# Two tiles of the key and value expansion in one double bank of PSUM

## Chip, cores and metric

The kernel runs on one core of a Trainium2 chip. The metric is the device time of one execution in microseconds (us). The kernel before takes 885.75 us, the median of three runs (884.52 to 885.99).

## What is computed

The reference is one step of a hybrid layer over 512 latent tokens and 128 context tokens, with a mLSTM head group (4 heads) and an attention head group (8 heads) side by side, then an output projection and an MLP. The part that the change touches is the expansion of the low-rank latent `ckv` (256 columns) to the keys and values of all eight attention heads:

```python
kv = (ckv @ w_kv_up).reshape(B, T, A_HEADS, A_NOPE + A_VDIM)
k_nope, v = kv[..., :A_NOPE], kv[..., A_NOPE:]
...
k = _rmsnorm(k, k_head_g)
```

It is done for the latent tokens, for a cache of 128 past tokens and for the context tokens: 768 rows, that is 6 blocks of 128.

## The kernel before

All of the kernel is one function, `hybrid_layer`, built with tile pools. A pool has a fixed number of buffers for each tag; a tile takes one, and the buffer comes free when every instruction that uses the tile is done. The tile framework puts in the semaphores, and it sets the order of each engine's instructions itself: by program order as priority, but an instruction that isn't ready in its own timeline (`schedule_with_timeline_sim=True`, line 1407) lets later ones go first. So the program text is not the order on the engines, and that order is fixed before the kernel runs.

**PSUM.** The pool `psd` (line 69, tag "d", function `psD`) has two buffers of 128x1024 f32, each two banks of 512. The pool `pss` (line 70, `psS`) has four buffers of one bank.

**The stages in program order.** The input projections (`group_n`, lines 490 to 506) accumulate five row blocks at once: blocks 0 and 1 are the two halves of one `psD` tile, blocks 2 and 3 those of another, block 4 is a `psS` tile. Then the four mLSTM heads follow (lines 794 to 798): `head_in` projects a head's queries, keys and gate; `mlstm` makes scores `s` and `c`, weights `W` and `p`, and numerators `n` (line 702); `mlstm_end` normalises and transposes (`den`, `hm`, `ht`, lines 766 to 790). Lines 801 to 814 transpose `ckv` into the split operands `kth` and `ktl`.

**The expansion** (lines 834 to 863) runs over two halves `hf` of the heads, and in each over six row blocks `i`. A tile `kvu{hf}{i}` takes six matmuls of 128x512 (line 846, through `mm3`, lines 486 to 488). Three readers empty it: ScalarE copies the keys to `kn` (line 848), ScalarE casts the values to `v` (line 109), VectorE subtracts to give the low part of `v` (line 110), while for the sixth block ScalarE's copy of the values to `vctx` (line 852) stands in place of the last two. ScalarE squares the keys (`sqk`, line 854) and VectorE sums them (`ssk`, line 855); both read only the copy. After the six blocks, VectorE takes the reciprocal root (lines 856 to 858) and GpSimd scales the keys (lines 860 and 861). The text below writes tile 3 for block 3 of the first half and tile h3 for block 3 of the second half. Each tile asks for a whole `psD` buffer of two banks and uses the first 512 columns.

The second half's value tile `v` (line 837) takes the SBUF buffer of `mv_u`, which the last mLSTM head still reads, so its casts can start only when the last `n` matmul is done.

**After it**, `qlt` (lines 867 to 873) transposes the query latent in three `psD` tiles, which ScalarE scales and casts; then come the query expansion `qu`, the conditioning products `ada`, attention (`head_q`, `head_k` and so on), the output projection and the MLP (`up`, `dn`). The first product of the MLP's first pair (lines 1223 to 1266) again puts two results, M1 and M2, in the halves of one `psD` tile: M1 is written and copied out by ScalarE (line 1256), and M2 is written into the other half by later matmuls.

Of the kernel before, what the change touches and what calls it, by code (L numbers as in the profile page):

```python
# [54 lines left out]
def hybrid_layer(ctx: ExitStack, tc: tile.TileContext, d, o):  # L55
# [19 lines left out]
    def U(name, dt=F32):  # L75
        return upool.tile([P, UNIT], dt, tag="u", name=name)
# [4 lines left out]
    def view(t, off, *shape):  # L81
        n = int(np.prod(shape))
        v = t[:, off:off + n]
        if len(shape) == 1:
            return v
        names = "abcd"[:len(shape)]
        return v.rearrange("p (%s) -> p %s" % (" ".join(names), " ".join(names)), **dict(zip(names, shape)))
# [5 lines left out]
    def Pp(name, dt=F32, n=T):  # L93
        return tp.tile([P, 646], dt, tag="pp", name=name, bufs=2)[:, :n]

    def sm(name, shape, dt=F32, bufs=2):
        return sp.tile(shape, dt, tag=name, name=name, bufs=bufs)

    def psD(name):
        return psd.tile([P, 1024], F32, tag="d", name=name)  # L100
# [7 lines left out]
    def split(hi, lo, src, eng=V):  # L108
        S.copy(hi, src)  # L109
        return eng.tensor_tensor(out=lo, in0=src, in1=f(hi), op=ALU.subtract)  # L110
# [89 lines left out]
    def wget(key, ahead=3):  # L200
        i = state["get"]
        assert chunks[i][0] == key, (chunks[i][0], key)
        wsplit(i + 1)
        wdma(i + 4)
        wsplit(i + ahead)
        state["get"] += 1
        return ready.pop(i)
# [137 lines left out]
    for what in ORD:  # L345
        if what == "x":
            i = state["x"]
# [15 lines left out]
    def rsqrt_v(y, x):  # L363

        n = x.shape[-1]
        t = sm("nwt", [P, 24], bufs=1)[:, :n]
        V.tensor_scalar(out=y.bitcast(I32), in0=x.bitcast(I32), scalar1=-0.5, scalar2=float(0x5F3759DF), op0=ALU.mult, op1=ALU.add)
        V.tensor_scalar(out=x, in0=x, scalar1=-0.5, scalar2=None, op0=ALU.mult)
        for _ in range(3):
            V.tensor_tensor(out=t, in0=y, in1=y, op=ALU.mult)  # L370
            V.tensor_tensor(out=t, in0=t, in1=x, op=ALU.mult)
            V.scalar_tensor_tensor(out=y, in0=t, scalar=1.5, in1=y, op0=ALU.add, op1=ALU.mult)
# [112 lines left out]
    def mm3(out, lh, ll, rh, rl, start, stop):  # L485
        PE.matmul(out, lhsT=lh, rhs=rh, start=start, stop=False)
        PE.matmul(out, lhsT=lh, rhs=rl, start=False, stop=False)
        PE.matmul(out, lhsT=ll, rhs=rh, start=False, stop=stop)
# [345 lines left out]
    for hf in range(2):  # L834
        ku = U(f"kn{hf}")
        kn = view(ku, 0, 6, 4, QK)
        vu = U(f"v{hf}", F32R)
        vv = view(vu, 0, 5, 4, P)
        hi, lo = wget(("kup", hf))
        ssk = sm("ssk", [P, 6, 4], bufs=1)  # L840
        rsk = sm("rsk", [P, 6, 4], bufs=1)
        for i in range(6):
            ps = psD(f"kvu{hf}{i}")[:, 0:512]
            for k in range(2):
                c = slice(k * 512, (k + 1) * 512)
                mm3(ps, kth[:, k, i * P:(i + 1) * P], ktl[:, k, i * P:(i + 1) * P], hi[:, c], lo[:, c], k == 0, k == 1)
            p4 = ps.rearrange("p (h c) -> p h c", h=4)
            S.copy(kn[:, i, :, 0:NOPE], p4[:, :, 0:NOPE])
            if i < 5:
                split(vv[:, i, :, 0:VD], vv[:, i, :, VD:P], p4[:, :, NOPE:P])  # L850
            else:
                S.copy(vctx[:, hf], p4[:, :, NOPE:P])
            sq = view(Pp(f"sqk{hf}{i}"), 0, 4, NOPE)
            S.activation(out=sq, in_=kn[:, i, :, 0:NOPE], func=AF.Square)
            V.tensor_reduce(out=ssk[:, i, :], in_=sq, axis=AX.X, op=ALU.add)
        V.tensor_tensor(out=ssk, in0=ssk, in1=ssr.unsqueeze(2).broadcast_to([P, 6, 4]), op=ALU.add)
        V.tensor_scalar(out=ssk, in0=ssk, scalar1=1.0 / QK, scalar2=EPS, op0=ALU.mult, op1=ALU.add)
        rsqrt_v(rsk.rearrange("p a b -> p (a b)"), ssk.rearrange("p a b -> p (a b)"))
        for k in range(4):
            G.tensor_tensor(out=kn[:, :, k, 0:NOPE], in0=kn[:, :, k, 0:NOPE], in1=rsk[:, :, k:k + 1].broadcast_to([P, 6, NOPE]), op=ALU.mult)  # L860
            G.tensor_tensor(out=kn[:, :, k, NOPE:QK], in0=krr, in1=rsk[:, :, k:k + 1].broadcast_to([P, 6, ROPE]), op=ALU.mult)
        kn_u.append(kn)
        v_u.append(vv)
# [10 lines left out]
    for hf in range(2):  # L874
# [4 lines left out]
        for i in range(NT):  # L879
            ps = (psS if i % 2 else psD)(f"qu{hf}{i}")  # L880
# [276 lines left out]
    for m in OUT_ORDER:  # L1157
        if m == 0:
            ps = ps_first
            with tc.issue_after(factors.ins):  # L1160
                mmT(ps, w_first, MHv, MLv, KT, 4)
        elif m == OUT_ORDER[1]:
            ps = psD(f"wo{m}")
# [4 lines left out]
        else:  # L1168
            ps = psD(f"wo{m}")
# [113 lines left out]
    for g in range(NG):  # L1283
# [19 lines left out]
        for h, m2 in downs(g):  # L1303
            w = wnext(("down", h, m2))
            for m in (2 * m2, 2 * m2 + 1):
                ps = psD(f"dn{h}{m}")
# [108 lines left out]
```

## Time and profile before

| what | value |
|---|---|
| median of three runs | 885.75 us |
| the profiled execution | 885.93 us |
| its span, first to last instruction | 883.8 us |
| TensorE busy | 856.6 us, 97% |
| VectorE busy | 615.9 us, 70% |
| ScalarE busy | 436.6 us, 49% |
| GpSimd busy | 297.2 us, 34% |
| expansion, first to last matmul start | 229.4 to 261.9 us |

The table is read against the span: the 2.13 us between span and execution lie around the program. Matmuls overlap, so the busy time of TensorE is an upper view of its work; what counts for the change is where TensorE stands idle, and which event ends the idle time.

### The profile page before, as it was taken

The page shows a single profiled execution, that of the slowest core. Times are in us where ns is not written, and L with a number is a line of the kernel's source. Part 1 is how long each engine was busy: PE and PEld are TensorE (multiplying, and loading weights), DVE is VectorE, ACT ScalarE, POOL GpSimd, SP SyncE. Part 2 cuts the span into 40 slices and gives each one's busy share as a digit, 9 for nine tenths or more (in the row PEclk, how much of TensorE's full clock was granted, in tenths as well). Part 3 has the DMA queues.
Part 4 walks back from the last instruction along what each step waited for, and adds up shares of the span by engine and source line. Part 5 has one row for each costly group of instructions (what it writes and reads, how often), then busy time and mean ns, then how long its engine had stood idle before and what let it go on. Part 6 is the DMA issues. An engine that isn't in the chain of part 4 may idle for free.

```text
span 883.8 us, 15202 instructions
## 1 busy us (share of the span) xinstructions
PE 856.6 (97%) x5805; PEld 801.8 (91%) x5805; DVE 615.9 (70%) x1226; ACT 436.6 (49%) x959; POOL 297.2 (34%) x301
## 2 busy tenths in 40 slices
PE   6999999999889999999989999999999999999998
PEld 5689889999778677889989999999999999999998
DVE  2654733646787889977898587595876949678663
ACT  3424425545864688955557253361544517254540
POOL 3100113322333576743753152241514215152300
PEclk9999999999999999999999999999999999999999
DMA  9742853231316200322141312122122221412132
GB/s 358 307 145 61 281 185 89 63 102 48 99 57 239 96 1 1 120 72 72 49 144 45 99 49 96 49 96 96 49 96 88 80 73 57 134 50 73 48 102 90
DMA packets 22328, 89.63 MB, mean 101 GB/s; under 512 B 3144, under 2 KB 3944, under 8 KB 18928
## 3 DMA queue, kind: packets, MB, share of 16 engines
q1 hardware_dynamic: 19440, 81.95, 26.8%
q0 software_dynamic: 1664, 4.26, 1.7%
q10 hardware_dynamic: 1152, 2.46, 0.7%
q8 instruction: 46, 0.75, 0.4%
q14 instruction: 26, 0.21, 0.1%
HBM read 85.33 MB, written 3.32 MB: 100 GB/s over the span
## 4 chain that ended last, share of the span: by engine, by line
PE 84%; DVE 8%; DMA 3%; ACT 3%; issue 1%; POOL 0%; SPq 0%; DVEq 0%; ACTq 0%; POOLq 0%
PE dn L637 25%; PE qk L637 6%; PE wo L637 5%; PE mo L637 3%; PE ada L389 2%; PE pv L1013 2%; DMA st<-in_w_ada 2%; PE n L702 2%; PE up8M L1235 1%; PE up12M L1235 1%; PE up13M L1235 1%; PE up15M L1235 1%; PE up14M L1235 1%; PE up11M L1235 1%; PE up9M L1235 1%; PE up7M L1235 1%
## 5 line engine op out<-in xcount | busy, mean ns | idle before, releaser
L109 ACT CAST wh<-st 128x1024 fp32r<-128x1024 f32 (+4 forms) x69 | 69.3, 1007 | 101.1 <-PE dn L637 32.9
L1118 DVE SCALAR_TENSOR_TENSOR xr<-dn,modT,xr 128x320 f32<-128x320 f32 x64 | 35.3, 551 | 107.3 <-PE dn L637 107.3
L637 PE MATMUL dn<-fh,wh 128*128 128x320 f32 x448 | 102.7, 310 | 0.2 <-ACT fh L1278 0.2
L110 DVE TENSOR_TENSOR wl<-st,wh 128x1024 fp32r<-128x1024 f32 (+4 forms) x67 | 83.3, 1246 | 27.8 <-ACT wh L109 26.8
L637 PE MATMUL dn<-fh,wl 128*128 128x320 f32 x448 | 102.0, 309 | 0.0
L637 PE MATMUL dn<-fl,wh 128*128 128x320 f32 x448 | 98.7, 309 | 0.0
L109 ACT CAST wu<-S 128x512 fp32r<-128x512 f32 x64 | 38.1, 616 | 98.5 <-issue 92.3
L637 PEld LDWEIGHTS dn<-fh,wh 128*128 128x128 f32 x448 | 74.8, 188 | 2.1 <-PE dn L637 1.6
L637 PEld LDWEIGHTS dn<-fh,wl 128*128 128x128 f32 x448 | 75.0, 188 | 0.0
L637 PEld LDWEIGHTS dn<-fl,wh 128*128 128x128 f32 x448 | 74.1, 188 | 0.0
L1273 POOL TENSOR_TENSOR r<-r,rbs 128x320 f32<-128x320 f32 x32 | 37.4, 1180 | 106.9 <-DVE r L1251 106.9
L110 DVE TENSOR_TENSOR wu<-S,wu 128x512 fp32r<-128x512 f32 x64 | 57.4, 906 | 1.1 <-ACT wu L109 0.9
L1277 ACT ACTIVATE r<-r 128x192 f32<-128x192 f32 (+2 forms) x96 | 40.8, 465 | 26.0 <-DVE r L1251 17.1
L729 POOL TENSOR_TENSOR W<-ngb,mask 128x128 f32<-128x128 f32 x40 | 19.5, 501 | 66.5 <-DVE p L739 33.2
L1280 DVE TENSOR_TENSOR fl<-r,fh 128x320 fp32r<-128x320 f32 x56 | 38.1, 699 | 3.0 <-ACT r L1279 3.0
L1004 POOL TENSOR_TENSOR tot<-tot,p 128x512 f32<-128x512 f32 x24 | 37.2, 1550 | 5.9 <-ACT p L986 3.9
L109 ACT CAST wu<-pair 128x512 fp32r<-128x512 f32 x24 | 14.1, 615 | 43.8 <-PE dn L637 41.6
L110 DVE TENSOR_TENSOR pu<-p,pu 128x512 fp32r<-128x512 f32 x32 | 33.0, 1046 | 2.5 <-ACT pu L109 2.5
L219 POOL TENSOR_TENSOR S<-st,st 128x512 f32<-128x512 f32 x8 | 13.0, 1627 | 60.1 <-DVE wu L110 60.1
L1013 PE MATMUL pv<-pu,v 128*128 128x512 f32 x80 | 29.1, 427 | 2.1 <-DVE pu L110 2.0
L637 PE MATMUL wo<-mh,wh 128*128 128x320 f32 x128 | 29.6, 311 | 0.7 <-DVE xr L1120 0.7
L637 PE MATMUL qk<-hh,wl 128*128 128x320 f32 x128 | 29.9, 312 | 0.0
(487 smaller groups left out, 2437.6 us busy)
## 6 DMA issues: line engine op xcount, KB each, us to landing
st<-in_w_ada SPq DMA_DIRECT2D x16, 1024.0 KB, 5.4
st<-in_w_down SPq DMA_DIRECT2D x32, 512.0 KB, 3.4
ad<-in_w_ada SPq DMA_DIRECT2D x8, 1024.0 KB, 17.2
st<-in_w_up SPq DMA_DIRECT2D x16, 512.0 KB, 3.7
pair<-in_w_up SPq DMA_DIRECT2D x16, 512.0 KB, 4.9
st<-in_w_qko SPq DMA_DIRECT2D x12, 512.0 KB, 3.6
st<-in_w_out SPq DMA_DIRECT2D x8, 512.0 KB, 3.5
x<-in_x SPq DMA_DIRECT2D x4, 640.0 KB, 6.8
```

The lines of the kernel that those rows point to most:

```text
L109: S.copy(hi, src)
L110: return eng.tensor_tensor(out=lo, in0=src, in1=f(hi), op=ALU.subtract)
L389: PE.matmul(ps[32 * j:32 * j + 32, 0:n], lhsT=sz[:, 2 * q + k, :], rhs=w[:, k, c], start=q == 0, stop=q == 3, tile_position=(0, 32 * j))
L637: PE.matmul(out[:, hf * 512:hf * 512 + HT], lhsT=wt[:, c], rhs=xt[k][:, hf * HT:(hf + 1) * HT], start=k0 == 0 and n == 0, stop=k1 == nk an ...
L729: G.tensor_tensor(out=W[:, dg:dg + P], in0=nb_[dr][:, j * P:(j + 1) * P], in1=mask[:, dr, :], op=ALU.add)
L1004: G.tensor_tensor(out=tot[h], in0=first, in1=pj, op=ALU.add)
L1013: PE.matmul(pacc[h], lhsT=v_u[hf][:, j, hh_, :], rhs=w, start=j == 0 and k == 0, stop=j == 4 and k == 1)
L1118: V.scalar_tensor_tensor(out=xr[m][:, 0:HT], in0=ps[:, 0:HT], scalar=modT[:, gi_ + m, 0:1], in1=xr[m][:, 0:HT], op0=ALU.mult, op1=ALU.add)
L1235: PE.matmul(ps, lhsT=w[:, c], rhs=b[k], start=k == 0 and w is hi and b is bh, stop=k == 3 and w is lo)
L1273: E.tensor_tensor(out=t, in0=t, in1=rbs[:, c], op=ALU.mult)
L1277: S.activation(out=t[:, c0:c1], in_=t[:, c0:c1], func=AF.Relu, bias=r[n][:, w:w + 1])
L1280: V.tensor_tensor(out=FL[n][:, c], in0=t, in1=f(FH[n][:, c]), op=ALU.subtract)
```

## The change

Two consecutive row blocks take the two halves of one `psD` tile. The matmuls, the readers and their number stay as they are, and no load, store or SBUF tile is touched.

```diff
         for i in range(6):
-            ps = psD(f"kvu{hf}{i}")[:, 0:512]
+            if i % 2 == 0:
+                pair = psD(f"kvu{hf}{i}")
+            ps = pair[:, i % 2 * 512:i % 2 * 512 + 512]
             for k in range(2):
```

## Rows read from the trace of the kernel before

**Rows 1.** The page, part 1: busy time and share of the span.
```profile
PE 856.6 (97%) x5805; PEld 801.8 (91%) x5805; DVE 615.9 (70%) x1226; ACT 436.6 (49%) x959; POOL 297.2 (34%) x301
```

**Rows 2.** The waits of TensorE: us in total, times, longest us.
```profile
PE kvu L486 <- DVE v L110: 2.8, 3, 1.3
...
PE up0M L1235 <- ACT r L1256: 1.6, 1, 1.6
```

**Rows 3.** The timeline of TensorE: start us, us, instruction, [idle before <-releaser].
```profile
234.36 0.49 PE L760 MATMUL pc<-mv_u,kw 128*128 128x129 f32 x2 [1.41 <-ACT kw L757]
...
241.79 0.50 PE L486 MATMUL kvu<-wh,kth 128*128 128x512 f32 x1 [1.26 <-DVE v L110]
...
255.59 0.50 PE L486 MATMUL kvu<-wh,kth 128*128 128x512 f32 x1 [0.93 <-DVE v L110]
...
259.28 0.50 PE L486 MATMUL kvu<-wh,kth 128*128 128x512 f32 x1 [0.65 <-DVE v L110]
...
260.78 0.39 PE L486 MATMUL kvu<-wh,kth 128*128 128x512 f32 x1
...
262.16 0.74 PE L870 MATMUL qlt<-ident,ql_u 128*128 128x128 f32 x5
...
264.80 0.77 PE L870 MATMUL qlt<-ident,ql_u 128*128 128x128 f32 x5 [0.64 <-ACT qlt L872]
...
290.86 0.84 PE L937 MATMUL Tk<-ident,kn 128*96 128x128 f32 x6
```

**Rows 4.** The timeline around the first projection, TensorE and VectorE, tile `mv`.
```profile
57.38 0.40 PE L488 MATMUL mv<-wh,hl 128*128 128x512 f32 x1
...
58.08 0.40 PE L488 MATMUL mv<-wh,hl 128*128 128x512 f32 x1
...
58.52 3.28 DVE L514 COPY mv_u<-mv 128x512 f32<-128x512 f32 x5 [0.97 <-PE mv L488]
```

**Rows 5.** The timeline around the second projection, TensorE and VectorE, tile `kv`.
```profile
74.03 0.30 PE L488 MATMUL kv<-wh,hl 128*128 128x304 f32 x1
...
74.45 0.30 PE L488 MATMUL kv<-wh,hl 128*128 128x304 f32 x1
...
74.79 0.47 DVE L531 COPY kvs<-kv 128x304 f32<-128x304 f32 x1 [1.10 <-PE kv L488]
...
75.81 0.86 DVE L531 COPY kvs<-kv 128x304 f32<-128x304 f32 x2 [0.18 <-ACT ck_u L532]
```

**Rows 6.** The timeline at the MLP's first pair, ScalarE and TensorE.
```profile
452.58 0.43 ACT L1256 COPY r<-up0M 128x322 f32<-128x322 f32 x1
...
453.06 1.74 PE L1235 MATMUL up0M<-B,wu 128*128 128x322 f32 x10 [1.60 <-ACT r L1256]
```

**Rows 7.** The timeline of VectorE in the second half of the expansion.
```profile
255.93 0.41 DVE L110 TENSOR_TENSOR v<-kvu,v 128x256 fp32r<-128x256 f32 x1
...
259.46 0.42 DVE L110 TENSOR_TENSOR v<-kvu,v 128x256 fp32r<-128x256 f32 x1
...
261.66 0.42 DVE L110 TENSOR_TENSOR v<-kvu,v 128x256 fp32r<-128x256 f32 x1 [0.72 <-ACT v L109]
...
262.33 1.06 DVE L787 TENSOR_SCALAR hm<-hm,rsh 128x128 f32<-128x128 f32 x5
```

**Rows 8.** The timeline of ScalarE in the same stretch and just behind it.
```profile
254.69 0.65 ACT L109 CAST v<-kvu 128x256 fp32r<-128x256 f32 x2 [2.98 <-PE n L702]
...
260.98 0.37 ACT L848 COPY kn<-kvu 128x256 f32<-128x256 f32 x1 [0.24 <-PE kvu L488]
261.25 0.38 ACT L109 CAST v<-kvu 128x256 fp32r<-128x256 f32 x1
...
263.95 0.80 ACT L872 ACTIVATE qlt<-qlt,small 128x640 f32<-128x640 f32 x1
264.77 0.73 ACT L109 CAST qth<-qlt 128x640 fp32r<-128x640 f32 x1
```

**Rows 9.** The timeline of GpSimd: the last scaling of the first half's keys.
```profile
255.94 0.51 POOL L861 TENSOR_TENSOR kn<-krr,rsk 128x192 f32<-128x192 f32 x1
```

## The prediction

> **What bounds the kernel now.** I read the page first: TensorE is busy for 856.6 of 883.8 us [rows 1], so an edit elsewhere pays only where it shortens one of TensorE's idle stretches. The list of TensorE's waits comes next. One of its largest entries belongs to the tiles of the change: three waits of 2.8 us together, ended by VectorE's subtraction of `v` [rows 2]. The timeline places them: 1.26 us ahead of 241.79, 0.93 ahead of 255.59, 0.65 ahead of 259.28. Two neighbours belong to the same stretch: 1.41 us ahead of 234.36, where TensorE waits for ScalarE's `kw` with two tiles of the expansion waiting to be emptied and no buffer for a third, and 0.64 ahead of the third `qlt` [rows 3]. That is 4.89 us of idle time, 0.55% of the run, and everything the edit could reach directly. A difference under about 0.2% (1.8 us) can't be told from no change in a measurement of this kernel.
>
> Before the change, two tiles are under way at most: tile i starts when tile i-2 has been read for the last time. The waits above are that rule at work.
>
> **The change, part by part.** It adds and removes no matmul, copy, cast, subtraction or DMA, so each queue has the same work. What it alters is who waits for whom. Two buffers of two halves could hold four tiles; whether four are ever under way hangs on one question: may TensorE write one half of a `psD` tile while ScalarE or VectorE reads the other half? Three places of this kernel already use the halves that way.
>
> First, the `mv` projection. In its last round each row block takes three matmuls, block 0 before block 1, the two being halves of one tile. Block 0's last matmul ends at 57.38 + 0.40 = 57.78, block 1's at 58.08 + 0.40 = 58.48. VectorE has been idle for 0.97 us and starts to read block 0 at 58.52 [rows 4], 0.74 us after its half was complete and 0.04 after the other half was. Second, `kv`: block 0 is complete at 74.33, block 1 at 74.75, and VectorE's read of block 0 starts at 74.79; its read of block 1 waits for ScalarE's read of block 0 [rows 5]. Third, and nearest to the case: M2 of the MLP's first pair is written into the half beside M1, and TensorE stands for 1.60 us until ScalarE's copy of M1 ends at 453.01, then starts at 453.06 [rows 6]. In all three the wait goes by the whole tile, not by the half: a read waits for writes to the other half, a read for a read of it, a write for a read of it.
>
> So tile 1 can't start beside the emptying of tile 0; it waits for all three of tile 0's readers, because they come earlier in the program and use the same `psD` tile. Each buffer becomes a chain, one of tiles 0, 1, 4, 5, the other of 2, 3, h0, h1, with h2, h3 behind 5 and h4, h5 behind h1. Within a chain one tile is written or emptied at a time. Two chains, so two tiles under way, as before. The engines take ready work out of program order, so I expect 0, 2, 1, 3, 4, h0, 5, h2 where it was 0, 1, 2, 3, 4, 5, h0, h1: the k-th tile waits for the emptying of the (k-2)th in both.
>
> The Trainium skill says otherwise: PSUM — Partial Sum Buffer, section "PSUM bank collisions raise a hardware error", asks for semaphores by bank and quadrant, and different banks don't collide. By that rule the two halves would be independent and four tiles could be under way; the rows of the three places speak against it for this kernel's waits.
>
> Now the terms. **Waits of 1.41, 1.26, 0.93 and 0.65 us:** each keeps its cause, with another tile in the role. Ahead of 234.36 tiles 0 and 2 are in flight in place of 0 and 1. At 241.79 it is h0 that waits for tile 3's subtraction. At 255.59 h1 waits for h0's, at 259.28 h4 for h1's. Term: 0.
>
> **The end of the second half.** Here the order can't be made up for. Before, h5 followed h4 without a gap, at 260.78. Now both are in one chain and nothing of the expansion is left beside them. h5 waits for h4's readers: keys copied at 260.98, values cast at 261.25 [rows 8], subtraction at 261.66 to 262.08 [rows 7]; h5 starts at about 262.12, 1.34 us late. The other buffer is free by then, since h3's subtraction ends at 259.88 [rows 7], so the first `qlt` moves ahead of h5 and its 0.74 us fill part of the gap [rows 3]. Left: +0.60. In return, by the time of the third `qlt` its buffer is free and ScalarE has done the first `qlt` long before, so its wait of 0.64 goes: -0.64. Together 0.0 us on TensorE's path.
>
> **What moves behind cover.** Tile 5 is written one place later (1.4 us), and so the first half's keys are scaled later than 255.94 + 0.51 = 256.45 [rows 9]. Their first reader is the transpose at 290.86 [rows 3]: 34 us of cover. If that were gone, the cost would be the 1.4 us. Loads are issued when TensorE or ScalarE frees their tiles, and those times move by tenths. Cost: 0.
>
> **What the trace doesn't show:** the new order itself, which is drawn up anew for all of the kernel behind the edit. Best case: the freer choice between tile 5 and h0 covers the 1.26 us. Worst case: no `qlt` ahead of h5, and 1.34 us. I take neither, being so close to zero on both sides, and keep -1.3 and +1.4 for the range.
>
> Sum: 885.93 for the profiled execution (span 883.8 and 2.13 around it) + 0.0 = 885.9; the median of the runs lies 0.18 lower, so 885.8.
>
> **The rivals.**
>
> *Faster: the halves are independent after all.* Then four tiles are under way. Tiles 2 and 3 fill the 1.41 us and the second half gets two tiles more ahead of the end of the mLSTM at 254.69 [rows 8]: 2 x 1.38 us of work (260.78 to 262.16) against 1.41 + 1.26 idle, so that end moves by 0.09. After it the last pair waits for h0 and h1 to be emptied, until 255.93 + 0.41 = 256.34 [rows 7], then takes 1.50 + 1.38 and ends at about 259.2 + 0.1 instead of 262.16. It saves 2.8 us: 882.9. For it: the 4.9 us are real, and the halves hold separate accumulations. Against it: the three places in rows 4 to 6. The skill's rule of the page named above would lead here. Chance 0.13.
>
> *Slower: the last pair stands alone behind other work.* If ScalarE takes the first `qlt`'s two operations, 0.80 + 0.73 us [rows 8], ahead of h4's cast, then h4's subtraction becomes ready 1.5 us later, after 263.1, and falls behind the five `hm` operations that VectorE runs from 262.33 to 263.39 [rows 7]. It then ends at 263.81 and h5 starts at 263.85 instead of 260.78: 3.07 us late, less the 0.74 of the moved `qlt`, so +2.3 us: 888.1. It decides as soon as the cast of h4 is queued behind the first of those ScalarE operations. For it: in the profile before, the subtractions of h2 and h3 already queue among such work. Against it: the cast belongs to earlier program text and has priority when it is ready. Chance 0.18.
>
> *The forecast: the change doesn't do what it says*, and two tiles remain under way. Chance 0.69.
>
> **How the numbers follow.** The likeliest case gives 885.8. With its bounds of -1.3 and +1.4, and some 0.3 for the measurement, it covers 884.2 to 887.5, which leaves out the faster rival at 882.9 and the slower one at 888.1, apart from partial cases of either, and little of the likeliest. The chances of faster by over 0.2%, no difference and slower by over 0.2% are those of the three cases.
>
> **What would show it.** In the profile after, the second tile of a pair should start only after the subtraction of the first: odd tiles' first matmuls 0.05 us or so behind VectorE's `v`, tiles 0 and 2 ahead of 1, the waits on `v` still near 2.8 us and one more ahead of h5, the `pc` wait still 1.4 us, and a first `qlt` ahead of the last expansion tile. I am wrong if four tiles' matmuls stand together at 229 to 236 us and the wait for `kw` is gone, or if the time between the last `n` matmul and the first `qu` shrinks by over 2 us.

## The result and the profile after

The changed kernel takes 892.54 us (median of 4 runs, 891.70 to 895.17), the kernel before beside it 885.87: a ratio of 1.0084 with a 95% interval of 1.0064 to 1.0104. Measured twice more it was 1.0062 (1.0042 to 1.0083) and 1.0044 (1.0027 to 1.0061). The forecast was 885.8, no change, with a range of 884.2 to 887.5; the change costs 4 to 7 us. Part of the width of that figure is TensorE's granted clock: in some traces it is at half for a few microseconds in the MLP's first pair, and some runs of every kernel here have a lower mean clock (0.990 to 0.996). The last batch of experiments is about that.

The page of the profiled execution (892.2 us, span 890.2 us), part 1, against [rows 1]:

```profile
PE 860.3 (97%) x5805; PEld 804.4 (90%) x5805; DVE 616.7 (69%) x1226; ACT 436.5 (49%) x959; POOL 296.7 (33%) x301
```

The counts are the same to the instruction, so no work was added; 6.4 us of span were. The list of TensorE's waits (us in total, times, longest) answers to [rows 2]:

```profile
PE kvu L486 <- DVE v L110: 5.3, 5, 1.6
...
PE up0M L1237 <- ACT r L1258: 2.1, 1, 2.1
```

The waits for VectorE's `v` went from three of 2.8 us together to five of 5.3. TensorE's timeline (start us, us, instruction, [idle before <-releaser]; lines behind the edit are two higher than before) shows which, against [rows 3]:

```profile
234.75 0.49 PE L760 MATMUL pc<-mv_u,kw 128*128 128x129 f32 x2 [1.41 <-ACT kw L757]
...
239.87 0.50 PE L486 MATMUL kvu<-wh,kth 128*128 128x512 f32 x1 [0.34 <-DVE v L110]
...
242.75 0.50 PE L486 MATMUL kvu<-wh,kth 128*128 128x512 f32 x1 [1.22 <-DVE v L110]
...
256.77 0.49 PE L486 MATMUL kvu<-wh,kth 128*128 128x512 f32 x1 [1.57 <-DVE v L110]
...
261.38 0.50 PE L486 MATMUL kvu<-wh,kth 128*128 128x512 f32 x1 [1.57 <-DVE v L110]
...
262.87 0.71 PE L872 MATMUL qlt<-ident,ql_u 128*128 128x128 f32 x5
264.23 0.50 PE L486 MATMUL kvu<-wh,kth 128*128 128x512 f32 x1 [0.65 <-DVE v L110]
...
266.62 0.77 PE L872 MATMUL qlt<-ident,ql_u 128*128 128x128 f32 x5 [0.19 <-ACT vctx L854]
...
268.36 0.77 PE L872 MATMUL qlt<-ident,ql_u 128*128 128x128 f32 x5 [0.97 <-ACT qlt L874]
```

The rows don't number the tiles; by the chains of the prediction, and by whose reader ends each wait, what stands ahead is in order of time: `pc`, with two tiles in flight (1.41, as before), 4 and h0 (0.34 + 1.22 for the 1.26 of before), h1 (1.57 for 0.93), h4 (1.57 for 0.65), h5 (0.65, new), and the second and third `qlt` (0.19 + 0.97 for 0.64). That is 3.0 us more idle time; a wait of 0.21 ahead of an `n` matmul at 252.16 is gone, so 2.8 us are left. I measure all kernels from here on by two ways in their traces: **the short way**, from the start of the first `kvu` matmul to that of the first `qu` matmul (36.14 us before, 265.55 - 229.41; 39.33 after), and **the long way**, to the first `up0M` matmul of the MLP (217.01 before, 220.84 after). What runs ahead of the first `kvu` is the same program in both and differs by up to 2.6 us from trace to trace.

The larger part of the growth, 1.56 us, is at h1 and h4, whose waits have the cause that the prediction named: the subtraction of the tile before them in the chain. VectorE's timeline shows why they are longer:

```profile
255.56 0.82 DVE L770 SCALAR_TENSOR_TENSOR den<-num 128x5 f32<-128x5 f32 x1
256.31 0.41 DVE L110 TENSOR_TENSOR v<-kvu,v 128x256 fp32r<-128x256 f32 x1
...
257.36 2.32 DVE L779 TENSOR_SCALAR hm<-num,den 128x128 f32<-128x128 f32 x5
259.60 1.39 DVE L780 SCALAR_TENSOR_TENSOR hm<-num,den,hm 128x128 f32<-128x128 f32 x5
260.91 0.41 DVE L110 TENSOR_TENSOR v<-kvu,v 128x256 fp32r<-128x256 f32 x1
```

The subtraction that h1 waits for stands behind `den`, which takes 0.82 us. The five `hm` products take 2.32 us. In the kernel before the same two take 0.18 and 1.07:

```profile
255.02 0.18 DVE L770 SCALAR_TENSOR_TENSOR den<-num 128x5 f32<-128x5 f32 x1
...
256.50 1.07 DVE L779 TENSOR_SCALAR hm<-num,den 128x128 f32<-128x128 f32 x5
```

The subtraction of `v` that h4 waits for is queued behind the products. And beside all of them, from 254.25 to 259.40, GpSimd now scales the first half's keys, which before was over at 256.45 [rows 9]:

```profile
254.25 0.84 POOL L862 TENSOR_TENSOR kn<-kn,rsk 128x384 f32<-128x384 f32 x1 [3.48 <-issue]
...
258.88 0.52 POOL L863 TENSOR_TENSOR kn<-krr,rsk 128x192 f32<-128x192 f32 x1
```

GpSimd's own instructions are no longer than before (0.84 and 0.51 to 0.52 us). Only VectorE pays. Taken one by one, the five products last 0.36, 0.56, 0.88, 0.56 and 0.28 us, and each of the first four ends 0.08 us behind the end of a GpSimd instruction; the third, for one:

```profile
258.08 0.84 POOL L862 TENSOR_TENSOR kn<-kn,rsk 128x384 f32<-128x384 f32 x1
258.12 0.88 DVE L779 TENSOR_SCALAR hm<-num,den 128x128 f32<-128x128 f32 x1
```

### The profile page after: what moved, and what is told of

Read it like the earlier page. It is cut to its first block, busy times and chain, and to the rows that moved or that the text cites. A ratio compares the mean times of both kernels' runs of the same rounds, so it can differ in the third digit from the quotient of the medians.

```text
span 890.2 us, 15198 instructions
## 1 busy us (share of the span) xinstructions
PE 860.3 (97%) x5805; PEld 804.4 (90%) x5805; DVE 616.7 (69%) x1226; ACT 436.5 (49%) x959; POOL 296.7 (33%) x301
## 4 chain that ended last, share of the span: by engine, by line
PE 82%; DVE 8%; DMA 4%; ACT 3%; issue 2%; POOL 0%; SPq 0%; DVEq 0%; POOLq 0%; ACTq 0%
PE dn L637 25%; PE qk L637 6%; PE wo L637 5%; PE mo L637 2%; DMA st<-in_w_ada 2%; PE ada L389 2%; PE pv L1015 2%; PE n L702 2%; PE up1M L1237 2%; PE up12M L1237 1%; PE up8M L1237 1%; PE up14M L1237 1%; PE up11M L1237 1%; PE up7M L1237 1%; PE up5M L1237 1%
## 5 line engine op out<-in xcount | busy, mean ns | idle before, releaser
L110 DVE TENSOR_TENSOR wu<-S,wu 128x512 fp32r<-128x512 f32 x64 | 59.4, 937 | 2.4 <-ACT wu L109 2.2
```

## The experiments

Theory S: the scaling, which by the later tile 5 starts 2.6 us later (24.46 us behind the first `kvu` in place of 21.90), falls beside VectorE's `hm` products and makes them slow, which holds up h1 and h4; the end of the second half costs the rest. Theory C: the chains of tiles themselves, or the order of the work, cost it. Theory K: the change itself brings the half clock in the MLP's first pair, and that is a good part of the loss. All figures in one table; ratios are to the kernel before on the same chip.

| kernel | short way | long way | five `hm` | median, us | ratio (95%) |
|---|---|---|---|---|---|
| before | 36.14 | 217.01 | 1.07 | 885.87 | 1 |
| after | 39.33 | 220.84 | 2.32 | 892.54 | 1.0084 (1.0064-1.0104) |
| e1_pair_no_scale | 37.79 | 219.30 | 1.07 | 888.30 | 1.0026 (1.0007-1.0045) |
| e2_before_no_scale | 35.76 | 216.07 | 1.07 | 885.63 | 0.9993 (0.9979-1.0008) |
| e3_pair_first_half | 37.89 | 218.52 | 2.32 | 887.04 | 1.0013 (0.9990-1.0035) |
| e4_pair_second_half | 37.59 | 219.42 | 1.07 | 887.36 | 1.0024 (1.0005-1.0042) |
| e10_pair_again | 39.14 | 220.69 | 2.32 | 892.45 | 1.0062 (1.0042-1.0083) |
| e11_pair_late_scale | 37.55 | 219.02 | 1.07 | 887.81 | 1.0019 (1.0003-1.0036) |
| e5_four_banks | 42.47 | 225.70 | 1.06 | 893.31 | 1.0077 (1.0055-1.0099) |
| e8_before_up_apart | 36.15 | 217.24 | 1.07 | 890.71 | 1.0046 (1.0031-1.0061) |
| e15_before_delay | 37.89 | 219.01 | 2.42 | 888.12 | 1.0025 (1.0009-1.0041) |
| e12_before_late_scale | 35.23 | 215.63 | 1.07 | 884.64 | 0.9986 (0.9968-1.0005) |
| e14_four_late | 38.59 | 222.00 | 1.06 | 891.22 | 1.0067 (1.0042-1.0093) |
| e16_pair_late_sep | 36.00 | 219.21 | 1.07 | 887.31 | 1.0011 (0.9997-1.0025) |
| e17_pair_third | 39.22 | 221.88 | 2.32 | 890.11 | 1.0044 (1.0027-1.0061) |
| e19_pair_late_again | 37.68 | 219.22 | 1.07 | 887.98 | 1.0023 (1.0006-1.0041) |
| e18_late_again | 35.25 | 216.72 | 1.07 | 884.86 | 0.9972 (0.9958-0.9987) |

The two ways are of one trace each. Where a program was traced again, the short way repeats within 0.2 us (after, e10 and e17; e11 and e19; e12 and e18), the long way only within 1.2 us (220.69 to 221.88 for the changed kernel), since TensorE's waits for loads of `in_w_ada` differ. So tenths count in the short way and not in the long one.

### Without the first half's scaling

Left out of the changed kernel (e1) and, as a control, of the one before (e2); the first half's keys stay unscaled in both:

```diff
-        for k in range(4):
+        for k in range(4 if hf else 0):
             G.tensor_tensor(out=kn[:, :, k, 0:NOPE], ...)
```

> The changed kernel with the first half's key scaling on GpSimd left out (eight operations); the order on TensorE is that of the changed kernel. Theory S (the scaling came later and now runs into VectorE's work behind the mLSTM): the five hm operations fall from 2.32 to about 1.07 us, the wait ahead of h1 from 1.57 to about 0.9, ahead of h4 from 1.57 to about 0.6; the way from the first expansion matmul to the first qu matmul is 1.3 to 1.7 us shorter than the 39.3 of the changed kernel. Theory C (the chain inside a pair alone costs the time): those waits stay near 1.57 and the way stays at 39.3. Time by S about 891, by C 892.5.

> The same eight operations left out of the kernel before: the control. Theory S: there the scaling ended at 256.4, ahead of the hm operations, and met only two small operations of VectorE; so the way from the first expansion matmul to the first qu matmul, 36.1 us, falls by 0 to 0.5. Time 885.4 to 885.9. Were it to fall by 1.5 too, leaving out the work would be worth that in itself and the first experiment would say nothing of the change.

```profile
256.25 1.07 DVE L779 TENSOR_SCALAR hm<-num,den 128x128 f32<-128x128 f32 x5
```

In e1 `hm` is back at 1.07, and the short way is 1.54 us less than after's, as S had it. In e2 the way falls by 0.38: the kernel before already had a little of the same neighbourhood. Between e1 and e2 there are still 2.03 us, so of the change's 3.19 us the scaling accounts for 1.16 net. The waits in the roles of h1 and h4 are the same in e1 and e2 (0.92 and 0.24). What e1 has more than e2 stands mostly ahead of h5 (0.96 us, while after has 0.65 and e2 none) and ahead of the two `qlt` (0.19 + 0.97 against 0.48).

### Pairs in one half only

```diff
-            if i % 2 == 0:
+            if i % 2 == 0 or hf == 1:    # e4: hf == 0
                 pair = psD(f"kvu{hf}{i}")
-            ps = pair[:, i % 2 * 512:i % 2 * 512 + 512]
+            h_ = 0 if hf == 1 else i % 2 * 512
+            ps = pair[:, h_:h_ + 512]
```

> Pairs in the first half only. Theory S: tile 5 is chained behind tile 4, the scaling is late and meets the hm operations, so this half of the change carries the two long waits: the way from the first expansion matmul to the first qu matmul is 38.0 to 38.6 us (before 36.1, changed 39.3), time 887.8 to 888.5 if nothing else follows. Theory C: the chain costs where no other tile is left, at the end of the second half, which is unpaired here: 36.1 to 36.5 us, time about 886.

> Pairs in the second half only. Theory S: the scaling is as early as before; only the wait of 0.65 ahead of h5 and some 0.3 at the query transposes remain: the way from the first expansion matmul to the first qu matmul is 36.9 to 37.3 us, time about 887 if nothing follows. Theory C: this half carries the loss: 38.5 to 39.3 us, 888.5 to 889. Theory K (the other half of the loss comes from the lower clock at the MLP's first pair, and from the order behind the expansion, which is here that of the changed kernel): 2 us more in either case, with a stretch at 0.5 of the full clock near 459 us.

```profile
261.68 0.50 PE L486 MATMUL kvu<-wh,kth 128*128 128x512 f32 x1 [0.65 <-DVE v L110]
...
265.80 0.77 PE L873 MATMUL qlt<-ident,ql_u 128*128 128x128 f32 x5 [0.97 <-ACT qlt L875]
```

The rows are of e4. The two halves are two separate losses: +1.75 us of short way for the first, +1.45 for the second, 3.20 together, and the whole change has 3.19. Only the first has the slow `hm`; only the second has the late h5 and `qlt`. The second costs more than S had (36.9 to 37.3 us) and less than C had (38.5 to 39.3). By the times each alone is near the edge of what can be measured.

### The scaling moved, with all of the work kept

```diff
+    ssk2 = sm("ssk", [P, 2, 6, 4], bufs=1)
+    rsk2 = sm("rsk", [P, 2, 6, 4], bufs=1)
     for hf in range(2):
...
-        V.tensor_scalar(out=ssk, in0=ssk, ...)
-        rsqrt_v(rsk..., ssk...)
...
+    V.tensor_scalar(out=ssk2, in0=ssk2, ...)
+    rsqrt_v(rsk2..., ssk2...)
+    for hf in range(2):
+        kn, rsk = kn_u[hf], rsk2[:, hf]
         for k in range(4):
             G.tensor_tensor(out=kn[:, :, k, 0:NOPE], ...)
```

> The changed kernel itself once more, beside the others on one chip. By theory S (the stage pays by itself) the way from the first matmul of the expansion to the first of the query expansion is 39.3 us, 3.2 above the kernel before, the stretch behind it up to the first up0M 0.6 us longer, and the median 3.8 us above before: a ratio of 1.0043; a granted clock of half in the first MLP pair comes in some of its runs as in some of before's, and adds some 3 us only there. By rival K (the change itself brings the half clock, by the longer wait ahead of the second part of up0M) nearly all of its runs have it, and the ratio is 1.007 or more.

> The changed kernel with all of its work, but both halves' key scaling stands behind the second half, on one inverse root for both; GpSimd scales nothing while VectorE runs the five hm operations. By theory S they take 1.07 us again in place of 2.32, the waits ahead of h1 and h4 fall from 1.57 each to about 0.9 and 0.2 to 0.7, and the way from the first kvu to the first qu is 37.6 to 38.0, as where the scaling was left out (37.8). If what was left out helped by something else than the neighbourhood of the scaling and hm, the way stays at 39 or more. GpSimd then works until some 7 us later than before, by about 287 us, and the keys are first read at about 291: no cost by that.

e10 is the changed kernel once more, e11 the same with the edit. The edit moves VectorE's reciprocal root along with GpSimd's scaling, so it takes a little more out of the stage than e1 does. Late scaling takes 1.6 to 1.8 us off the changed kernel's short way (39.14 and 39.33 against 37.55), and 4.6 us off its median on the same chip, part of which is clock (below). VectorE of e11 in the stretch of the slow group, then TensorE at h1, h4 and h5:

```profile
257.03 1.07 DVE L779 TENSOR_SCALAR hm<-num,den 128x128 f32<-128x128 f32 x5
258.02 1.40 DVE L780 SCALAR_TENSOR_TENSOR hm<-num,den,hm 128x128 f32<-128x128 f32 x5
259.33 0.42 DVE L110 TENSOR_TENSOR v<-kvu,v 128x256 fp32r<-128x256 f32 x1
```

```profile
256.51 0.50 PE L486 MATMUL kvu<-wh,kth 128*128 128x512 f32 x1 [0.92 <-DVE v L110]
...
259.81 0.50 PE L486 MATMUL kvu<-wh,kth 128*128 128x512 f32 x1 [0.24 <-DVE v L110]
...
262.97 0.50 PE L486 MATMUL kvu<-wh,kth 128*128 128x512 f32 x1 [0.95 <-DVE v L110]
```

The wait ahead of h4 is 0.24, less than the 0.65 of before; h5's has grown to 0.95. Both are as in e1, where the root had stayed in its place. The rest of the change's price stands at the end of the second half.

### The same neighbourhood made in the kernel before

If S is right, the slow `hm` can be made without any pair. Six extra scalings of the rotary part (overwritten with the same values) push the end of the eight back by some 3 us:

```diff
+        for k in ((0, 1, 2, 3, 0, 1) if hf == 0 else ()):
+            G.tensor_tensor(out=kn[:, :, k, NOPE:QK], in0=krr, ...)
         for k in range(4):
```

> The kernel before, TensorE's order and all tiles as they were, with one thing put in: GpSimd scales the rotary part of the first half's keys for six heads more (overwritten by the same values), 6 x 0.52 = 3.1 us, ahead of the eight scalings, which so fall at about 254.3 to 259.5 as in the changed kernel. By theory S the five hm operations take about 2.3 us in place of 1.07, the waits ahead of h1 and h4 grow to about 1.6 each, and the way from the first kvu to the first qu is 37.3 to 38.0 in place of 36.1. If the chain of tiles made them slow, and not GpSimd's neighbourhood, hm stays at 1.07 and the way at 36.1 to 36.3.

GpSimd, then VectorE, then TensorE of e15:

```profile
256.18 1.00 POOL L860 TENSOR_TENSOR kn<-krr,rsk 128x192 f32<-128x192 f32 x2
257.14 1.95 POOL L863 TENSOR_TENSOR kn<-krr,rsk 128x192 f32<-128x192 f32 x4
```

```profile
256.75 2.42 DVE L779 TENSOR_SCALAR hm<-num,den 128x128 f32<-128x128 f32 x5
259.09 1.39 DVE L780 SCALAR_TENSOR_TENSOR hm<-num,den,hm 128x128 f32<-128x128 f32 x5
```

```profile
255.84 0.50 PE L486 MATMUL kvu<-wh,kth 128*128 128x512 f32 x1 [1.35 <-DVE v L110]
...
260.87 0.50 PE L486 MATMUL kvu<-wh,kth 128*128 128x512 f32 x1 [1.98 <-DVE v L110]
```

The order on TensorE and the tiles are those of before, and `hm` takes 2.42 us. It ends at 259.17, 0.08 us behind GpSimd's last scaling (257.14 + 1.95 = 259.09), and the next VectorE group, 1.39 us, is as before. The short way grows by 1.75, the long by 2.00, the median by 2.06. This is the clearest of the runs: GpSimd's neighbourhood alone, without a pair, costs as much as pairs in the first half do (e3).

The Trainium skill has the rule for it, in SBUF — State Buffer, section "Who interferes with whom": VectorE and GpSimd share one pair of ports as an exclusive lock, `tensor_scalar` can enter a mode that takes it, and whoever issues first blocks the other for the whole instruction. The traces agree: products of 0.28 us each became up to 0.88 us in the changed kernel and end 0.08 us behind GpSimd's instructions, which kept their 0.84 us. The ports themselves are seen in no trace here.

### Four tiles under way

What the change was to allow, without a shared tile: four buffers of one bank each (e5), and the same with late scaling (e14). To make room, the pool `psd` is closed ahead of the stage and opened anew behind it.

```diff
+    psd_stack.close()
+    psk = kv_stack.enter_context(tc.tile_pool(name="psk", bufs=4, space=PSUM))
...
-            ps = psD(f"kvu{hf}{i}")[:, 0:512]
+            ps = psk.tile([P, 512], F32, tag="k", name=f"kvu{hf}{i}")
...
+    kv_stack.close()
+    psd = ctx.enter_context(tc.tile_pool(name="psd2", bufs=2, space=PSUM))
```

> The kernel before with four tiles of one bank each for the expansion in place of two of two banks: what the change was to allow, without a shared tile. If four under way are worth what the faster rival of the prediction said, tiles 0 to 3 run in one block, the 1.41 ahead of pc and the 0.65 ahead of h4 go, and the way from the first kvu to the first qu is 33.3, 2.8 less than before: a ratio of 0.997. If the emptying of more tiles at once puts copies and subtractions ahead of the mLSTM's own operations on ScalarE and VectorE, the wait for kw and the second half's end move out by as much, and the way is 35.5 to 37: a ratio of 1.000 at best.

> Four tiles of one bank each together with the late scaling: what four under way bring when GpSimd scales nothing beside VectorE. If the 42.5 us of the four tiles alone came from the scaling beside the hm operations (3.20 in place of 1.06) and from the half clock behind the 4.29 us for which TensorE then stood, both go and the way is 36.5 to 37.5. If the emptying of more tiles ahead of the mLSTM's own operations is what held TensorE up, it still stands for 2 us or more ahead of ht, and the way is 38 or more. To be worth its making it would have to be under 36.1.

Four tiles do run as one block, and the waits of 1.41 ahead of `pc` and 1.26 ahead of the fifth tile are gone. It is slower all the same, by 6.3 us of short way in e5, more than either expectation had, and 2.5 in e14. TensorE of e14, where the gaps are, and ScalarE from its first copy of a tile to the last of the five `dg` sums that `hm` waits for:

```profile
250.93 1.12 PE L789 MATMUL ht<-ident,hm 128*128 128x128 f32 x4 [3.74 <-DVE hm L788]
...
265.52 1.31 PE L879 MATMUL qlt<-ident,ql_u 128*128 128x128 f32 x10 [0.92 <-ACT vctx L857]
```

```profile
235.67 0.37 ACT L853 COPY kn<-kvu 128x256 f32<-128x256 f32 x1 [4.25 <-PE kvu L489]
...
246.78 0.77 ACT L853 COPY kn<-kvu 128x256 f32<-128x256 f32 x2
...
247.61 0.52 ACT L853 COPY kn<-kvu 128x256 f32<-128x256 f32 x1
...
248.47 0.46 ACT L782 ACTIVATE dg<-hm 128x128 f32<-128x128 f32 x1
```

With more tiles to empty, ScalarE puts their copies and squares among the third head's `dg` sums; the last of these starts 17.9 us behind the first `kvu` (248.47 - 230.55), against 11.8 before (241.16 - 229.41). A part of that is a later start: the four tiles' last matmuls stand together at the end of the block, and ScalarE's first copy comes 5.1 us behind the first `kvu`, against 2.8 before (232.21 - 229.41). TensorE runs ahead with the expansion and then stands for the mLSTM. In e5 it was worse, since GpSimd's scaling also fell beside the five products at L788 (3.20 us for 1.06).

Two more things cost time in these kernels. Behind the gap the granted clock was lower, 0.72 from 248 to 254 us in e14 and 0.53 and 0.62 from 248 to 260 us in e5; in all other traces it is 1.00 from 224 to 272 us. (A matmul of `s` takes 0.63 us there in e14 and 0.40 behind it.) And the first `qlt` starts only behind the last tile's `vctx`: the waits from there to the first `qu` are 0.92 + 0.71 + 0.83 us in e14, against 0.64 before. So the faster rival of the prediction, in this form, would not have been fast either. How much of the loss is the number of buffers, and how much the order inside the block, the clock and the pool opened anew, no run separates.

### M1 and M2 in tiles of their own

```diff
-        two_ = dict(M1="M2", M6="M7", M4="M3")
+        two_ = dict(M6="M7", M4="M3")
```

> The kernel before, with M1 and M2 of the first MLP pair in a tile of one bank each in place of the two halves of one tile. If waits go by the whole tile, as the prediction read from this place, the wait of 0.9 to 1.6 us for ScalarE's r ahead of the second part of up0M goes, and the time falls by 1 to 1.6 us: a ratio of 0.9985. If the wait was for something else that r stands for, it stays. If the half clock in this pair follows that wait, no run of this kernel has it, and the median falls by up to 3 us more; if not, it comes in some runs as before.

The wait for ScalarE's copy `r` [rows 6] is gone from the list, so it was a wait for the whole tile. Nothing is gained, against the expected 0.9985: TensorE takes other work first and then stands longer, at another place, and the granted clock, 1.00 up to 462 us and 0.91 from there to 468, was 0.52 in the 6 us that follow (0.50 is 1.2 GHz of 2.4):

```profile
467.99 2.25 PE L1235 MATMUL up0M<-B,wu 128*128 128x322 f32 x7 [3.46 <-DVE r L1251]
```

### Late scaling alone, and the last tile apart

e12 is the kernel before with late scaling. e16 is e11 with the last tile in a buffer of its own:

```diff
-            if i % 2 == 0:
+            if i % 2 == 0 or hf * 6 + i == 11:
                 pair = psD(f"kvu{hf}{i}")
-            ps = pair[:, i % 2 * 512:i % 2 * 512 + 512]
+            h_ = 0 if hf * 6 + i == 11 else i % 2 * 512
+            ps = pair[:, h_:h_ + 512]
```

> The kernel before with both halves' key scaling behind the second half, as in the changed kernel with late scaling, and all of the work. It takes the small rest of the same neighbourhood away: way from the first kvu to the first qu 35.7 to 35.8 in place of 36.1, a ratio of 0.9995. If GpSimd's later end holds up the transposes of the keys, it is slower than before by as much as they wait.

> The changed kernel with late scaling, and the last tile of the second half in a tile of its own; the other five pairs as changed. By theory S the wait of 0.65 to 0.95 ahead of h5 goes and the first qlt is read by ScalarE ahead of the third again, so of the 1.4 us that the late scaling left, 1.0 to 1.2 go: way 36.2 to 36.6, a ratio of 1.000. If the pairs cost something by themselves, it stays at 37 or more.

In e16 the wait ahead of h5 is gone, and the short way is 36.00, 1.55 less than e11's. Against e12, the same scaling without pairs, 0.77 us are left; 0.41 of them are the waits ahead of tiles 4 and h0 (0.44 + 1.22 for 1.25). But the long way is 219.21, 2.2 more than before. TensorE of e16 behind the stage:

```profile
290.88 1.07 PE L389 MATMUL ada<-st,sz 128*32 128x256 f32 x16 [1.73 <-DMA st<-in_w_ada]
...
296.76 1.07 PE L389 MATMUL ada<-st,sz 128*32 128x256 f32 x16 [0.60 <-DMA st<-in_w_ada]
```

TensorE stands there for 2.33 us for loads of `in_w_ada`; between the same two marks it was 0.63 before (0.47 + 0.16). All listed waits of that stretch come to 6.43 us in e16 and 4.78 in before, so 1.65 of the 2.34 us by which it is longer are waits. That they belong to this kernel isn't shown: the same program waited for these loads 0.70 us in after and 1.89 in e17, nothing in e12 and 1.26 in e18. The other 0.7 us stand in the changed kernel too (181.51 against 180.87, at 4.78 us of listed waits in both), and without the listed waits they stand in every trace with pairs in the second half (176.7 to 176.8 us) and in none of the other kernels with two tiles under way (175.8 to 176.2): there the `ada` products behind the stage come in another order (28 and 2 at first in after and e16, 32 together in before).

e12 has the shortest ways of all these kernels: 0.91 and 1.38 us less than before, and a median 1.42 lower. Of the 0.91, more than was expected, the scaling by itself explains 0.38 (e2); the rest comes with VectorE's root, moved too, or with the order. With e12 the 3.19 us of the change split up once more: 2.32 are the pairs with late scaling (e11 against e12), 1.78 the late scaling's gain in the changed kernel, less the 0.91 that it gains in the kernel before. By this split the neighbourhood is 0.87 net, by e1 and e2 it is 1.16, and the larger share is in both the pairs themselves. GpSimd's last scaling ends at 281.34 + 0.51 = 281.85, and the first transpose of keys starts at 290.81: the later end costs nothing.

```profile
281.34 0.51 POOL L866 TENSOR_TENSOR kn<-krr,rsk 128x192 f32<-128x192 f32 x1
```

### The clock in the MLP's first pair

In some traces TensorE's granted clock falls to half behind the idle stretches of the MLP's first pair, and in others with such stretches it doesn't; in after's own, the 6 us windows from 456 and 462 us (columns: busy time and count of PE, PEld, DVE, ACT, POOL, then PEclk, DMA share and GB/s):

```profile
450.00:456.00 6.00, 5.67 (x39) 5.41 (x37) 6.00 (x12) 4.01 (x8) 2.83 (x2) 1.00 0.93 315
456.00:462.00 6.00, 3.97 (x15) 3.16 (x15) 6.00 (x9) 3.03 (x8) 3.73 (x6) 0.73 0.39 158
462.00:468.00 6.00, 5.83 (x31) 5.83 (x32) 3.54 (x9) 1.77 (x4) 1.27 (x2) 0.70 0.00 0
```

The same two matmuls of `up0M` take 0.91 us there and 0.56 in the trace of before. From the first `up0M` matmul to the group of 24 it is 17.87 us against 15.81: 2.06 of the 6.4 us of span. Is that the change? The ratio of e10, 1.0062, lies between what S (1.0043) and K (1.007) had for it. Three kernels were run once more: the changed one (e17), e11 (e19), and e12 (e18).

> The changed kernel once more, for the share of its runs in which the granted clock fell (mean 0.996 or less over the run): 7 of its 12 runs so far, against 25 of 83 of the kernel before. If the half clock is chance and comes to every kernel alike, about 3 in 10 of these runs have it; if the change brings it, 6 in 10 again. The median is 6 us above before's by the second, 4 to 5 by the first.

> The changed kernel with late scaling once more, the same behind the expansion as the changed kernel: 3 of its 12 runs had the lower clock. If the scaling beside the hm operations has to do with the half clock 190 us later, its share stays at 2 to 3 in 10 while the changed kernel's is 6 in 10; if it is chance, the two shares come together. Median 1.5 us above before's.

> The kernel before with late scaling once more, to narrow its ratio, 0.9986 with an interval that reached 1.0005: if its way of 35.2 us from the first kvu to the first qu is what it gains, 0.9 us less than before and a few tenths in its waits for the loads of in_w_ada, the ratio is 0.998 to 0.999; if the first figure was scatter, 1.000.

A run counts as one with the lower clock when its mean is 0.996 or less. e17 had it in 1 of 7 runs, e19 in 3 of 12, the kernel before on that chip in 7 of 24. Over all batches it is 8 of 19 for the changed kernel and 32 of 107 for the one before: not to be told apart, so no run shows that the change brings it (theory K). The runs with a mean clock above 0.996 have medians of 890.31 (11 of the changed kernel) and 885.85 (75 of before): **the change itself costs 4.5 us**, and three of the first four runs had the low clock on top. The traces of its three profiled runs have long ways of 220.84, 220.69 and 221.88, on average 4.1 above before's 217.01 (217.24 in e8, the same program up to there); that is nearly all of it.

e19: 1.0023 (1.0006 to 1.0041). e18, the kernel before with late scaling: 884.86 against 886.15, **0.9972 (0.9958 to 0.9987)**, short way 35.25. It is faster than both kernels, by 0.3% than the one before; e12's interval had reached 1.0005.

## Why the prediction was wrong

- **Who waits for whom: right.** The halves of one tile don't overlap in use here. h5, the second half of a pair, starts at 264.23, 0.06 us after the subtraction of h4 ends (263.75 + 0.42), while four tiles of one bank each (e5) ran together. The order forecast, 0, 2, 1, 3, 4, h0, 5, h2, fits the trace as far as it can be read: the first half's last tile, known by its copy `vctx`, is the seventh that ScalarE empties and was the sixth before. The 1.41 us ahead of `pc` stayed.
- **"What moves behind cover", cost 0: the first step that failed.** It asked only who reads the scaled keys, and found 34 us of cover. The cover is real (e11 and e12 use some 25 us of it at no cost). But a moved instruction also has neighbours on the other engines: the scaling, 2.6 us later and not 1.4, fell beside `den` and stretched it by 0.64 us, and beside five products and stretched them by 1.25. A subtraction behind the first ended h1's wait, one behind the second h4's. In the changed kernel this costs 1.5 (e1) to 1.8 us (e11) of short way; in the reverse test it cost 1.75 (e15). Net of what the kernel before paid already it is 1.16 (e1 and e2), since without it h5 waits 0.3 us longer.
- **"Waits of 1.41, 1.26, 0.93 and 0.65: term 0".** The causes are as named; the sizes of three were not: 0.34 + 1.22 for 1.26, 1.57 for 0.93, 1.57 for 0.65. The last two are the step above.
- **"The end of the second half", together 0.0: the second step that failed.** One term hit, the other had the wrong sign. h5 is 0.65 late (forecast 0.60). The third `qlt`'s wait was to go (-0.64), since "ScalarE has done the first `qlt` long before". It became 0.19 + 0.97, so +0.52. ScalarE of after:

```profile
265.93 0.37 ACT L850 COPY kn<-kvu 128x256 f32<-128x256 f32 x1 [1.89 <-PE kvu L488]
266.19 0.38 ACT L854 COPY vctx<-kvu 128x256 f32<-128x256 f32 x1
266.46 0.85 ACT L109 CAST wh<-st 128x768 fp32r<-128x768 f32 x1
267.19 0.43 ACT L856 ACTIVATE sqk<-kn 128x256 f32<-128x256 f32 x1
267.51 0.80 ACT L874 ACTIVATE qlt<-qlt,small 128x640 f32<-128x640 f32 x1
```

  ScalarE stood idle for 1.89 us with the first `qlt` complete since about 263.6, because in its fixed order h5's two copies, a cast of weights and a square come first; it reads that `qlt` at 267.51. The slower rival feared `qlt` ahead of the tile's readers; it was the other way round, and cost as well. This half of the loss is e4: +1.45 us of short way for a forecast of 0.0.
- **The range.** Its upper bound, +1.4, took in one of the two losses. Their sum and the stretch behind were outside it, with the clock (892.54) and without (890.31). The rival on the slower side named another place and 2.3 us.

Open: the 0.6 us behind the first `qu` at the same listed waits, which come with the pairs of the second half. The other order stands beside it in the traces, but no run changed that order alone.

## What to carry to other kernels

When an edit moves an instruction of GpSimd that nobody waits for, look at what VectorE runs in its new place, not only at who reads its result: two instructions off the critical path can be each other's delay, and TensorE pays. More buffers are not a gain by themselves: with four tiles under way ScalarE emptied tiles ahead of what TensorE needed next, and the whole was slower. In a fixed order, "ready long before" says nothing until it is seen what stands ahead on that engine.

## What the runs showed of the hardware

VectorE's `tensor_scalar` of 128x128 took 0.28 us alone and up to 0.88 us beside GpSimd's `tensor_tensor` of 128x384, a `scalar_tensor_tensor` on five columns 0.82 us in place of 0.18, and GpSimd lost nothing: I had expected contention to be shared. In the changed kernel and in e15 a stretched product ends 0.08 us behind a GpSimd instruction. And in the same stretch of the MLP's first pair TensorE was granted 1.00 in some traces and half for some 6 us in others, behind idle stretches of similar length (1.60 us ahead of 453.06 before, at full clock; 0.90 and 0.93 us in e10, at half).
